# A two-layer recurrent trunk: the chunk phase's matrix products held to the program's order on TensorE

## The chip, the cores and the metric

The kernel runs on one core of a Trainium2 chip. The metric is the device time of one execution in microseconds (us), on the slowest core, which here is the only one. Five engines work beside each other: TensorE (PE, with PEld for its weight loads), VectorE (DVE), ScalarE (ACT), GpSimd (POOL) and SyncE (SP). Each executes its own list of instructions strictly in the order in which the list was built; engines wait for each other by semaphores.

## The reference, cut to what matters

Two layers over x (1024 frames of 1024 float32 values), each as x + RMSNorm(mixer(RMSNorm(x))). Layer 0 has two recurrent mixers in parallel (RG-LRU and HGRN2). Layer 1, where the change is, is RWKV-7 time mixing with 16 heads of 64:

```
r, k, v, g = projections of the mixed input        # g is the gate
decay, iclr = low-rank projections
kk = k * k_k, normalised per head;  k = k * (1 + (iclr - 1) * k_a)
for t in frames:                                   # state: 64 x 64 per head
    sa    = state @ (-kk_t)
    state = state * decay_t + sa (x) (kk*iclr)_t + v_t (x) k_t
    y_t   = state @ r_t
y = groupnorm(y) * ln_w + ln_b + bonus
out = (y * silu(g)) @ w_out                        # then RMSNorm and x +
```

## The kernel before, in words

The program runs layer 0, its output, the projections of layer 1 (r, k, v and the low-rank ones) and a preparation of the keys and queries one after the other. Then comes `chain_phase`, the last third of the time, on which the change acts. It works on 16 chunks of 64 frames and has these kinds of work, each a Python generator that issues a piece of it per step:

- **The solves** (`solve_pairs`, `invert`, lines 1294 to 1306). Each chunk needs the inverse of a triangular 64x64 matrix per head. The diagonal blocks are solved by DVE alone, by substitution: a product of a row (1294, 1303; output `PR`) and a sum (1297, 1306; output `YP`), 544 instructions in all, two pairs of chunks interleaved. They need only POOL's scaled blocks `BL`.
- **The merge** (`merge(ch)`). It joins the solved blocks: a DVE transpose (1331), 16 small PE products `pi` (1337), an ACT copy, 16 more (1346), and a DMA of the result, from which the chunk later loads its inverse `YTc` (`values(ch)`, which also loads the chunk's values into `SV`).
- **The gram products** (`gram(ch)`). Two halves, each of 8 products `pg` on PE (1415) and four masked copies on DVE, into `GM` (1420) and `RB` (1421). Then POOL scales the keys `BK` (1424), PE transposes them (`pt`, 1429) and ACT copies them out as `NK`.
- **The chain** (`chain(ch)`), the recurrence itself. Four links on PE, each of 16 products of 64x64: `pc` from `SV` and `GM` (1442), beside it `py` (1447); `pc` from the inverse and `B` (1457), after ACT has copied B; `pc` from `NK` (1464). DVE adds that to the decayed state, two instructions `SV<-pc,se` (1466), which gives the next chunk's `SV`; call that of chunk c SV(c). Then `py` from `RB` and `SV` (1469) gives the chunk's output y.
- **The gate pieces** (`pieces`, `gpiece`, `dense_n`). 32 pieces of the projection of g, of 24 products each (184 to 186, output `po`), with a sigmoid on ACT and a product on DVE (1020). They are the fill of chunks 0 to 8 and depend on nothing in the chain.
- **The output** (`project(tt)`, 1536 to 1538). 8 tiles of 128 frames, each of 2 x 24 products; they are the fill from chunk 9 on. Tile tt needs chunks 2tt and 2tt + 1, each normed (`norm`, on DVE, ACT and POOL) and turned by four PE transposes (`turn`, 1518, output `pq` or `pe`) into `yh` and `yl`.

The main loop interleaves these in the program's text: for each of a chunk's five chain steps it issues a step of the chain, 6 steps of the solves and two of merges (`background(6)`), a step of the next chunk's gram and one of the fill. From chunk 8 on the solves are all issued.

That text does not set the order on the engines. A scheduler does, when the program is built: it simulates the program, and each engine takes, among the instructions that are ready, the one with the highest priority, which is the one stated first; `high_priority(offset=100)` raises the chain and the gram from chunk 14 on, and `offset=400` the last norm and turn. An instruction that isn't ready in that simulation is overtaken by later ones that are. Where two products use the same PSUM bank in turn (`BANKS`: `pt`, `pq` and `pi` share one; `pc` has two, `py` one, `po` two, `pg` and `pe` share two), the later one waits until the earlier one has been read.

Of the kernel before, what the change touches and what calls it, by code (L numbers as in the profile page):

```python
# [16 lines left out]
P = 128  # L17
# [28 lines left out]
class Net:  # L46
# [74 lines left out]
    def weights(self, units):  # L121

        self.wp = self.ctx.enter_context(self.pool("wp", 4))
        self.order, self.queue = list(units), []

    def load_unit(self, first=False):
        nc, i = self.nc, self.order.pop(0)
# [47 lines left out]
    def dense_n(self, w, uh, ul, tt):  # L175

        nc = self.nc
        ps = self.dps()[:, 0:256]
        sl = slice(tt % 4 * P, (tt % 4 + 1) * P)
        for k in range(KT):  # L180
            a, b = uh[tt // 4][k][:, sl], ul[tt // 4][k][:, sl]
            c = slice(k % 4 * 256, (k % 4 + 1) * 256)
            h, l = w[k // 4][0][:, c], w[k // 4][1][:, c]
            nc.tensor.matmul(ps, lhsT=a, rhs=h, start=(k == 0), stop=False)  # L184
            nc.tensor.matmul(ps, lhsT=a, rhs=l, start=False, stop=False)  # L185
            nc.tensor.matmul(ps, lhsT=b, rhs=h, start=False, stop=(k == KT - 1))  # L186
        return ps

    def rstd(self, pool, ss, n, scale, eps):
# [833 lines left out]
    def chain_phase(self, cx, mp, vg, n):  # L1023


        nc, a = self.nc, self.a
        both = lambda x, y: ((x[0], y[0]), (x[1], y[1]))
        self.mp = mp
        self.psb = cx.enter_context(self.pool("psb", 1, space=PSUM))
        self.nd = 0  # L1030

        def dps():
            self.nd += 1
            return self.bank("pd" if self.nd % 2 else "pe")
# [12 lines left out]
        self.SV, self.YTc, self.G, self.Y, self.yd = {}, {}, {}, {}, [self.dram.tile([P, HALF], F32, name=f"yd{i}") for i in range(16)]  # L1047
        g0, g1 = (self.mix_parts(mp, 3, th, nc.gpsimd) for th in range(2))
        for i in range(n):
            next(vg)  # L1050
            self.background(5)
            if i >= n - 8:
                next(g0)
        self.chain_consts()
        self.values(0)
        nc.gpsimd.memset(self.SV[0][0:64, 0], 0.0)
        nc.gpsimd.memset(self.SV[0][64:128, 1], 0.0)
        for _ in self.gram(0):
            pass
        self.dps = lambda: self.bank("po")  # L1060

        def output():
            for tt in range(8):
                yield from self.project(tt)

        self.fill = self.pieces(self.gpiece, *both(g0.parts, g1.parts))
        for ch in range(16):
            gr = iter(())
            if ch == 8:
                while self.solves:  # L1070
                    self.background(8)
                ivx.close()
                self.gp = cx.enter_context(self.pool("gp", 2))
                self.output_consts()
                self.W = {}
            if ch == 9:
                self.turn(0)
                self.turn(1)
                for _ in self.fill:
                    pass  # L1080
                self.fill = output()
            if 0 < ch < 15:
                self.values(ch + 1)
                gr = self.gram(ch + 1)
            steps = self.chain(ch)
            for i in range(5):
                with self.tc.high_priority(offset=100) if ch >= 14 else ExitStack():
                    if next(steps, True) is not None:
                        break
                self.background(6)  # L1090
                if ch == 0 and i < 2:
                    for _ in range(4):
                        next(g1)
                if ch == 0 and i == 1:
# [218 lines left out]
    def merge(self, ch):  # L1313
# [20 lines left out]
        for e in range(KT):  # L1334
            for h in range(2):
                r, r2 = slice(64 * h, 64 * h + 32), slice(64 * h + 32, 64 * h + 64)
                nc.tensor.matmul(ps[r2, e, 0:32], lhsT=A12[r, e, :], rhs=X1[r, e, :], start=True, stop=True)
        for h in range(2):
            r2 = slice(64 * h + 32, 64 * h + 64)
            nc.scalar.copy(F[r2], ps[r2, :, 0:32])  # L1340
# [2 lines left out]
        for e in range(KT):  # L1343
            for h in range(2):
                r, r2 = slice(64 * h, 64 * h + 32), slice(64 * h + 32, 64 * h + 64)
                nc.tensor.matmul(ps[r, e, 0:32], lhsT=F[r2, e, :], rhs=YT[r2, e, 32:64], start=True, stop=True)
# [52 lines left out]
    def gram(self, ch):  # L1399
# [10 lines left out]
        for eg in range(2):  # L1410
            ps = [self.bank("pg").rearrange("p (q t) -> p q t", t=P) for _ in range(2)]
            for q in range(4):
                for h in range(2):
                    hs = slice(64 * h, 64 * h + 64)
                    nc.tensor.matmul(ps[h][:, q, :], lhsT=BK[hs, eg * 4 + q, :], rhs=GM[hs, h, eg * 4 + q, :],  # L1415
                                     start=True, stop=True)
            for h in range(2):
                es = slice(eg * 4, eg * 4 + 4)
# [7 lines left out]
        for eg in range(2):  # L1426
            ps = self.bank("pt").rearrange("p (q t) -> p q t", t=P)
            for q in range(4):
                nc.tensor.transpose(ps[:, q, :], BK[:, eg * 4 + q, :], self.ident)
            nc.scalar.copy(NK[:, eg * 4:eg * 4 + 4, :], ps)  # L1430
        self.G[ch] = GM, RB, NK

    def chain(self, ch):
# [5 lines left out]
        pv = lambda ps: ps.rearrange("p (e v) -> p e v", v=64)  # L1439
        ps = pv(self.bank("pc"))  # L1440
        for e, h in eh:
            nc.tensor.matmul(ps[H[h], e, :], lhsT=GM[:, h, e, 0:64], rhs=SV[:, h, e, :], start=True, stop=True)
        B = self.cc[ch % 2].tile([P, KT, 64], F32, name="B")
        nc.scalar.copy(B, ps)
        py = pv(self.bank("py"))
        for e, h in eh:
            nc.tensor.matmul(py[H[h], e, :], lhsT=GM[:, h, e, 64:128], rhs=SV[:, h, e, :], start=(e == 0), stop=False,
                             skip_group_check=True)
        if ch < 15:
            se = self.cc[ch % 2].tile([P, KT, 64], F32, name="se")  # L1450
# [3 lines left out]
        yield  # L1454
        ps = pv(self.bank("pc"))
        for e, h in eh:
            nc.tensor.matmul(ps[H[h], e, :], lhsT=YT[H[h], e, :], rhs=B[H[h], e, :], start=True, stop=True)
        for h in range(2):
            nc.scalar.copy(SV[H[h], h], ps[H[h]])
        yield  # L1460
        if ch < 15:
            ps = pv(self.bank("pc"))
            for e, h in eh:
                nc.tensor.matmul(ps[H[h], e, :], lhsT=NK[:, e, H[h]], rhs=SV[:, h, e, :], start=True, stop=True)
            for h in range(2):
                nc.vector.tensor_add(self.SV[ch + 1][H[h], h], ps[H[h]], se[H[h]])  # L1466
        yield
        for e, h in eh:
            nc.tensor.matmul(py[H[h], e, :], lhsT=RB[H[h], e, :], rhs=SV[H[h], h, e, :], start=False, stop=(e == KT - 1),
                             skip_group_check=True)  # L1470
        y = self.cc[ch % 2].tile([P, HALF], F32, name="B")
        nc.scalar.copy(y, py.rearrange("p e v -> p (e v)"))
# [37 lines left out]
    def turn(self, ch):  # L1510
# [4 lines left out]
            self.yl = self.wp.tile([P, KT, P], F32R, name="yl", tag="wl")  # L1515
        ps = self.bank("pq" if ch < 12 else "pe")
        for q in range(4):
            nc.tensor.transpose(ps[:, q * P:(q + 1) * P], y[:, q * P:(q + 1) * P], self.ident)
        T = slice(64 * p, 64 * p + 64)
        self.split(ps.rearrange("p (k t) -> p k t", t=64), self.yh[:, :, T], self.yl[:, :, T])  # L1520

    def project(self, tt):
# [8 lines left out]
        for dh in range(2):  # L1531
            ds = slice(dh * HALF, (dh + 1) * HALF)
            po = self.bank("po")
            for k in range(KT):
                h, l = self.W[k, dh]
                nc.tensor.matmul(po, lhsT=yh[:, k, :], rhs=h, start=(k == 0), stop=False)  # L1536
                nc.tensor.matmul(po, lhsT=yh[:, k, :], rhs=l, start=False, stop=False)  # L1537
                nc.tensor.matmul(po, lhsT=yl[:, k, :], rhs=h, start=False, stop=(k == KT - 1))  # L1538
# [70 lines left out]
```

## Time and profile before

| what | value |
|---|---|
| median of 3 runs | 1861.41 us (1859.28 to 1864.62) |
| the profiled execution | 1867.26 us |
| its span, first to last instruction | 1865.6 us |
| mean granted clock of TensorE | 0.948 |
| PE busy | 1714.8 us (92%) |
| DVE busy | 1326.3 us (71%) |
| ACT busy | 776.5 us (42%) |
| POOL busy | 715.7 us (38%) |

The share of an engine is its mean over the whole span; the chunk phase, from about 1330 us on, differs from the rest. A line such as "L1466" is a line of the kernel, and "SV<-pc,se" means that an instruction writes the tile SV and reads pc and se. In the rows of a timeline the first column is the start in us from the beginning of the span, the second the duration. One product of 32-bit floats is executed in several passes and can show as more than one matmul in the profile. PEclk is the clock that TensorE was granted, as a share of full speed.

### The profile page before, as it was taken

What the parts mean: (1) busy time and instruction counts of PE and PEld (TensorE: products, weight loads), DVE (VectorE), ACT (ScalarE), POOL (GpSimd) and SP (SyncE); (2) the same over time, 40 slices, a digit from 0 to 9 for tenths busy, and PEclk for the clock granted to TensorE, in tenths of its full rate; (3) what the DMA queues carried; (4) which work ended last, traced back from release to release, by engine and by line L of the source; (5) the groups of instructions that cost most, each with busy time, mean ns of one, the idle gap of its engine ahead of it and who ended that gap; (6) DMA issues with size and microseconds to landing.
All of it is one profiled execution on the core that took longest, in us unless ns stands there. A gap on an engine that the chain in (4) does not pass through costs nothing. (4 is left out here: it accounts for less than half of the span.)

```text
span 1865.6 us, 34533 instructions
## 1 busy us (share of the span) xinstructions
PE 1714.8 (92%) x13394; PEld 1436.2 (77%) x13394; DVE 1326.3 (71%) x2605; ACT 776.5 (42%) x1484; POOL 715.7 (38%) x638
## 2 busy tenths in 40 slices
PE   8989989999899999999999999979788888898988
PEld 6879879788797777777878866659787777776766
DVE  6486484685946898835445486795999999658884
ACT  5222222323136655534545565677452322342321
POOL 5533333332332122365434243466353242464440
PEclk8989999999899999999999999979889989897989
DMA  5101101111012121265242256766244544755531
GB/s 183 46 24 35 57 24 69 45 33 38 24 63 85 57 69 67 100 225 198 94 141 89 92 136 159 166 172 187 87 128 128 164 134 114 213 185 161 172 101 63
DMA packets 177492, 201.80 MB, mean 108 GB/s; under 512 B 91440, under 2 KB 122416, under 8 KB 177328
## 3 DMA queue, kind: packets, MB, share of 16 engines
q1 hardware_dynamic: 176176, 195.39, 34.1%
q0 software_dynamic: 1152, 4.19, 0.7%
q8 instruction: 106, 1.74, 0.4%
q14 instruction: 58, 0.48, 0.1%
HBM read 136.28 MB, written 63.24 MB: 107 GB/s over the span
## 5 line engine op out<-in xcount | busy, mean ns | idle before, releaser
L135 POOL TENSOR_TENSOR wl<-w,wh 128x1024 fp32r<-128x1024 f32 x110 | 275.9, 2514 | 292.4 <-ACT wh L133 277.0
L160 PE MATMUL mm<-xh,wh 128*128 128x512 f32 x768 | 305.9, 399 | 1.2 <-ACT KK L1183 1.2
L162 PE MATMUL mm<-xh,wl 128*128 128x512 f32 x768 | 304.8, 397 | 0.0
L161 PE MATMUL mm<-xl,wh 128*128 128x512 f32 x768 | 303.9, 396 | 0.0
L184 PE MATMUL mm<-wh,xh 128*128 128x256 f32 x560 | 170.5, 305 | 5.0 <-ACT xh L149 3.3
L160 PEld LDWEIGHTS mm<-xh,wh 128*128 128x128 f32 x768 | 145.4, 189 | 36.8 <-issue 3.9
L162 PEld LDWEIGHTS mm<-xh,wl 128*128 128x128 f32 x768 | 145.5, 190 | 34.9 <-issue 4.6
L161 PEld LDWEIGHTS mm<-xl,wh 128*128 128x128 f32 x768 | 145.7, 190 | 33.5 <-issue 3.6
L186 PE MATMUL mm<-wh,xl 128*128 128x256 f32 x560 | 167.0, 301 | 4.7 <-DVE xl L150 3.2
L185 PE MATMUL mm<-wl,xh 128*128 128x256 f32 x560 | 165.8, 297 | 0.0
L133 ACT CAST wh<-w 128x1024 fp32r<-128x1024 f32 x112 | 117.4, 1050 | 116.2 <-PE mm L161 55.7
L1294 DVE TENSOR_TENSOR PR<-YP,BL 128x80 f32<-128x80 f32 (+21 forms) x240 | 125.3, 544 | 14.9 <-POOL BL L1276 12.4
L184 PEld LDWEIGHTS mm<-wh,xh 128*128 128x128 f32 x560 | 114.9, 205 | 8.2 <-ACT xh L149 3.8
L186 PEld LDWEIGHTS mm<-wh,xl 128*128 128x128 f32 x560 | 114.0, 205 | 7.0 <-DVE xl L150 4.0
L185 PEld LDWEIGHTS mm<-wl,xh 128*128 128x128 f32 x560 | 115.0, 205 | 0.7
L184 PE MATMUL po<-wh,xh 128*128 128x256 f32 x256 | 80.6, 315 | 2.1 <-DVE vg L1020 2.1
L185 PE MATMUL po<-wl,xh 128*128 128x256 f32 x256 | 78.8, 308 | 0.0
L186 PE MATMUL po<-wh,xl 128*128 128x256 f32 x256 | 77.9, 304 | 0.0
L420 DVE COPY_PREDICATED ST<-m_l,sm 64x128 f32<-64x128 uint8 x224 | 72.5, 337 | 5.5
L803 DVE SCALAR_TENSOR_TENSOR mix<-ut,vec,mix 128x512 f32<-128x512 f32 x64 | 58.1, 916 | 24.2 <-ACT mix L802 23.3
L1415 PE MATMUL pg<-GM,BK 64*128 64x128 f32 x512 | 61.9, 318 | 13.9 <-DVE RB L1421 6.6
L1453 POOL TENSOR_TENSOR se<-SV,egc 64x512 f32<-64x512 f32 x30 | 33.4, 1115 | 88.6 <-DVE SV L1466 87.2
(373 smaller groups left out, 4334.0 us busy)
## 6 DMA issues: line engine op xcount, KB each, us to landing
w<-in_W SPq DMA_DIRECT2D x112, 512.0 KB, 3.6
ard<-AR SPq DMA_DIRECT2D x16, 512.0 KB, 3.7
BK<-bkd SPq DMA_DIRECT2D x16, 512.0 KB, 4.9
vd<-vg SPq DMA_DIRECT2D x32, 256.0 KB, 2.8
GM<-ard SPq DMA_DIRECT2D x32, 256.0 KB, 4.4
x<-in_x SPq DMA_DIRECT2D x8, 512.0 KB, 10.1
mgd<-sgq SPq DMA_DIRECT2D x16, 256.0 KB, 2.2
ut<-mgd SPq DMA_DIRECT2D x16, 256.0 KB, 4.0
```

Source lines behind the costliest of these rows:

```text
L133: nc.scalar.copy(hi, w)
L135: (nc.vector if first else nc.gpsimd).tensor_sub(lo, w, hi.bitcast(F32))
L160: nc.tensor.matmul(ps, lhsT=wh[:, c:c + P], rhs=a, start=(k == 0), stop=False)
L161: nc.tensor.matmul(ps, lhsT=wh[:, c:c + P], rhs=b, start=False, stop=False)
L162: nc.tensor.matmul(ps, lhsT=wl[:, c:c + P], rhs=a, start=False, stop=(k == KT - 1))
L184: nc.tensor.matmul(ps, lhsT=a, rhs=h, start=(k == 0), stop=False)
L185: nc.tensor.matmul(ps, lhsT=a, rhs=l, start=False, stop=False)
L186: nc.tensor.matmul(ps, lhsT=b, rhs=h, start=False, stop=(k == KT - 1))
L420: nc.vector.copy_predicated(d, m, x)
L803: nc.vector.scalar_tensor_tensor(out, sh, self.v(f"mu{p}", k), out, ALU.mult, ALU.add)
L1294: nc.vector.tensor_mul(pr, fv(YP, yo, kd + [[48, 8], [1, n]]), fv(BL, ao + i, k0 + [[0, 8], [32, n]]))
L1415: nc.tensor.matmul(ps[h][:, q, :], lhsT=BK[hs, eg * 4 + q, :], rhs=GM[hs, h, eg * 4 + q, :], start=True, stop=True)
```

## The change

From the end of chunk 0's gram on, every product and every transpose on TensorE goes through `self.mm` or `self.tr`, which hand the instruction to `keep_in_program_order`. That adds to it an ordering edge to the instruction that PE was given just before it: the scheduler may no longer place it ahead of that one. The edge is between instructions of one engine, so it costs no semaphore; it changes nothing but the place in the list. The other engines stay free: DVE, ACT, POOL and SP are still scheduled by priority among what is ready.

```diff
+        self.mm, self.tr = self.nc.tensor.matmul, self.nc.tensor.transpose
...
         self.dps = lambda: self.bank("po")

+        pin = self.tc.keep_in_program_order
+        self.mm, self.tr = (lambda *a, f=f, **k: pin(f(*a, **k)) for f in (nc.tensor.matmul, nc.tensor.transpose))
+
...
-            nc.tensor.matmul(ps, lhsT=a, rhs=h, start=(k == 0), stop=False)
+            self.mm(ps, lhsT=a, rhs=h, start=(k == 0), stop=False)
...
-                nc.tensor.transpose(ps[:, q, :], BK[:, eg * 4 + q, :], self.ident)
+                self.tr(ps[:, q, :], BK[:, eg * 4 + q, :], self.ident)
```

The first line stands in `weights`, the lambda in `chain_phase`, the products shown in `dense_n` and `gram`. The same replacement is made for all other products of `dense_n`, `merge`, `gram`, `chain`, `turn` and `project`. The lines of the kernel shift by one behind the first edit and by four behind the second; pinned products carry the line of the lambda, 1064.

What it moves, in the built lists (a row is an instruction or a group of like ones; a number behind a name, as in `xh_13085`, is that of a buffer).

PE, where chunk 0's chain starts, before: its products `pc` and `py` come one or a few at a time between gate pieces (`po`), a merge (`pi`) and the next gram (`pg`).

```order
L184 MATMUL po<-wh,xh_13085 128x256
L185 MATMUL po<-wl,xh_13085 128x256
L186 MATMUL po<-wh,xl_13086 128x256
L184 MATMUL po<-wh,xh_13134 128x256
L1442 MATMUL pc<-SV,GM 64x64
L1447 MATMUL py<-SV,GM 64x64
L1346 MATMUL pi<-YT_11967,A_12712 32x32 x16
L1415 MATMUL pg<-GM,BK 128x128 x4
L185 MATMUL po<-wl,xh_13134 128x256
L186 MATMUL po<-wh,xl_13135 128x256
L184 MATMUL po<-wh,xh_13183 128x256
L185 MATMUL po<-wl,xh_13183 128x256
```

The same place after: the chain's 16 products `pc` and 16 `py` stand in one piece, behind the inversion products of chunks 2 and 3 and the key transposes, and the first gate pieces of the phase come after them.

```order
L1419 MATMUL pg<-GM,BK 128x128 x4
L1341 MATMUL pi<-X_13232,A_13071 32x32 x16
L1341 MATMUL pi<-X_13234,A_13082 32x32 x16
L1350 MATMUL pi<-YT_11966,A_13071 32x32 x16
L1350 MATMUL pi<-YT_11967,A_13082 32x32 x16
L1433 MATMUL pt<-ident,BK 128x128 x8
L1064 MATMUL pc<-SV,GM 64x64 x16
L1064 MATMUL py<-SV,GM 64x64 x16
L1064 MATMUL po<-wh,xh_12925 128x256
L1064 MATMUL po<-wl,xh_12925 128x256
L1064 MATMUL po<-wh,xl_12926 128x256
```

DVE around SV(4), before: the solves' rows 1294 and 1297 stand on both sides of it (410 of the 544 ahead of it), between gate products and gram masks.

```order
L1294 TENSOR_TENSOR PR<-YP,BL 128x208
L1294 TENSOR_TENSOR PR<-YP,BL 128x40
L1020 TENSOR_TENSOR vg<-po,vg 128x256
L1297 TENSOR_REDUCE YP<-PR 128x2x8
L1297 TENSOR_REDUCE YP<-PR 128x8
L1466 TENSOR_TENSOR SV<-pc,se 64x512 x2
L1294 TENSOR_TENSOR PR<-YP,BL 128x224
L1294 TENSOR_TENSOR PR<-YP,BL 128x48
L1420 TENSOR_TENSOR GM<-pg,gm 64x512
L1421 TENSOR_TENSOR RB<-pg,gm 64x256
L1297 TENSOR_REDUCE YP<-PR 128x2x8
```

After: 543 of the 544 solve rows (1298, 1301 and their fellows) stand ahead of SV(4), and the masks follow behind the last.

```order
L1301 TENSOR_REDUCE YP<-PR 128x2x8
L1298 TENSOR_TENSOR PR<-YP,BL 128x240
L1301 TENSOR_REDUCE YP<-PR 128x2x8
L1021 TENSOR_TENSOR vg<-po,vg 128x256
L1298 TENSOR_TENSOR PR<-YP,BL 128x256
L1470 TENSOR_TENSOR SV<-pc,se 64x512 x2
L1301 TENSOR_REDUCE YP<-PR 128x2x8
L1424 TENSOR_TENSOR GM<-pg,gm 64x512
L1425 TENSOR_TENSOR RB<-pg,gm 64x256
L1424 TENSOR_TENSOR GM<-pg,gm 64x512
L1425 TENSOR_TENSOR RB<-pg,gm 64x256
```

PE ahead of the last turn, before: the last output chain `py` (1469) is followed by 48 output products, of which the first rows are shown, and then the transposes `pe<-ident,B` of chunk 15's turn.

```order
L1518 MATMUL pe<-ident,yn 128x128 x8
L1469 MATMUL py<-SV,RB 64x64 x16
L1536 MATMUL po<-xh_16588,yh 128x512
L1537 MATMUL po<-xl_16589,yh 128x512
L1536 MATMUL po<-xh_17039,yh 128x512
L1537 MATMUL po<-xl_17040,yh 128x512
L1538 MATMUL po<-xh_16588,yl 128x512
L1536 MATMUL po<-xh_16592,yh 128x512
L1537 MATMUL po<-xl_16593,yh 128x512
L1538 MATMUL po<-xh_16592,yl 128x512
```

After, from the turn of chunk 14 (`pe<-ident,yn`) on: behind `py` stand 12 output products, of which the first rows are shown, and then the turn of chunk 15.

```order
L1064 MATMUL po<-xh_17053,yl 128x512
L1064 MATMUL pe<-ident,yn 128x128 x4
L1064 MATMUL py<-SV,RB 64x64 x16
L1064 MATMUL po<-xh_17106,yh 128x512
L1064 MATMUL po<-xl_17107,yh 128x512
L1064 MATMUL po<-xh_17106,yl 128x512
L1064 MATMUL po<-xh_17110,yh 128x512
L1064 MATMUL po<-xl_17111,yh 128x512
```

The last of the twelve, and the turn:

```order
L1064 MATMUL po<-xh_17120,yh 128x512
L1064 MATMUL po<-xl_17121,yh 128x512
L1064 MATMUL po<-xh_17120,yl 128x512
L1064 MATMUL pe<-ident,B 128x128 x4
L1064 MATMUL po<-xh_16588,yh 128x512
```

Of the 48 products that stood between this `py` and the turn, 12 stand there now; the other 36 stand ahead of `py`. Behind the turn stand 48 products in both.

More of the change, by code (lines that the diff above doesn't have):

```diff
@@ L183, in dense_n @@
             h, l = w[k // 4][0][:, c], w[k // 4][1][:, c]
-            nc.tensor.matmul(ps, lhsT=a, rhs=h, start=(k == 0), stop=False)
-            nc.tensor.matmul(ps, lhsT=a, rhs=l, start=False, stop=False)
-            nc.tensor.matmul(ps, lhsT=b, rhs=h, start=False, stop=(k == KT - 1))
+            self.mm(ps, lhsT=a, rhs=h, start=(k == 0), stop=False)
+            self.mm(ps, lhsT=a, rhs=l, start=False, stop=False)
+            self.mm(ps, lhsT=b, rhs=h, start=False, stop=(k == KT - 1))
         return ps
@@ L1336, in merge @@
                 r, r2 = slice(64 * h, 64 * h + 32), slice(64 * h + 32, 64 * h + 64)
-                nc.tensor.matmul(ps[r2, e, 0:32], lhsT=A12[r, e, :], rhs=X1[r, e, :], start=True, stop=True)
+                self.mm(ps[r2, e, 0:32], lhsT=A12[r, e, :], rhs=X1[r, e, :], start=True, stop=True)
         for h in range(2):
@@ L1345, in merge @@
                 r, r2 = slice(64 * h, 64 * h + 32), slice(64 * h + 32, 64 * h + 64)
-                nc.tensor.matmul(ps[r, e, 0:32], lhsT=F[r2, e, :], rhs=YT[r2, e, 32:64], start=True, stop=True)
+                self.mm(ps[r, e, 0:32], lhsT=F[r2, e, :], rhs=YT[r2, e, 32:64], start=True, stop=True)
         for h in range(2):
@@ L1414, in gram @@
                     hs = slice(64 * h, 64 * h + 64)
-                    nc.tensor.matmul(ps[h][:, q, :], lhsT=BK[hs, eg * 4 + q, :], rhs=GM[hs, h, eg * 4 + q, :],
+                    self.mm(ps[h][:, q, :], lhsT=BK[hs, eg * 4 + q, :], rhs=GM[hs, h, eg * 4 + q, :],
                                      start=True, stop=True)
@@ L1441, in chain @@
         for e, h in eh:
-            nc.tensor.matmul(ps[H[h], e, :], lhsT=GM[:, h, e, 0:64], rhs=SV[:, h, e, :], start=True, stop=True)
+            self.mm(ps[H[h], e, :], lhsT=GM[:, h, e, 0:64], rhs=SV[:, h, e, :], start=True, stop=True)
         B = self.cc[ch % 2].tile([P, KT, 64], F32, name="B")
@@ L1446, in chain @@
         for e, h in eh:
-            nc.tensor.matmul(py[H[h], e, :], lhsT=GM[:, h, e, 64:128], rhs=SV[:, h, e, :], start=(e == 0), stop=False,
+            self.mm(py[H[h], e, :], lhsT=GM[:, h, e, 64:128], rhs=SV[:, h, e, :], start=(e == 0), stop=False,
                              skip_group_check=True)
@@ L1456, in chain @@
         for e, h in eh:
-            nc.tensor.matmul(ps[H[h], e, :], lhsT=YT[H[h], e, :], rhs=B[H[h], e, :], start=True, stop=True)
+            self.mm(ps[H[h], e, :], lhsT=YT[H[h], e, :], rhs=B[H[h], e, :], start=True, stop=True)
         for h in range(2):
@@ L1463, in chain @@
             for e, h in eh:
-                nc.tensor.matmul(ps[H[h], e, :], lhsT=NK[:, e, H[h]], rhs=SV[:, h, e, :], start=True, stop=True)
+                self.mm(ps[H[h], e, :], lhsT=NK[:, e, H[h]], rhs=SV[:, h, e, :], start=True, stop=True)
             for h in range(2):
@@ L1468, in chain @@
         for e, h in eh:
-            nc.tensor.matmul(py[H[h], e, :], lhsT=RB[H[h], e, :], rhs=SV[H[h], h, e, :], start=False, stop=(e == KT - 1),
+            self.mm(py[H[h], e, :], lhsT=RB[H[h], e, :], rhs=SV[H[h], h, e, :], start=False, stop=(e == KT - 1),
                              skip_group_check=True)
@@ L1517, in turn @@
         for q in range(4):
-            nc.tensor.transpose(ps[:, q * P:(q + 1) * P], y[:, q * P:(q + 1) * P], self.ident)
+            self.tr(ps[:, q * P:(q + 1) * P], y[:, q * P:(q + 1) * P], self.ident)
         T = slice(64 * p, 64 * p + 64)
@@ L1535, in project @@
                 h, l = self.W[k, dh]
-                nc.tensor.matmul(po, lhsT=yh[:, k, :], rhs=h, start=(k == 0), stop=False)
-                nc.tensor.matmul(po, lhsT=yh[:, k, :], rhs=l, start=False, stop=False)
-                nc.tensor.matmul(po, lhsT=yl[:, k, :], rhs=h, start=False, stop=(k == KT - 1))
+                self.mm(po, lhsT=yh[:, k, :], rhs=h, start=(k == 0), stop=False)
+                self.mm(po, lhsT=yh[:, k, :], rhs=l, start=False, stop=False)
+                self.mm(po, lhsT=yl[:, k, :], rhs=h, start=False, stop=(k == KT - 1))
                 if k == 3:
```

## Prediction

> **What bounds the kernel now.** I read the page first, then the busy time by stretch, then VectorE's timeline and groups, then TensorE's timeline for the price of one product, and last the waits. From the page: the totals, and the slices of the two busy engines and of the clock.
>
> ```profile
> PE 1714.8 (92%) x13394; PEld 1436.2 (77%) x13394; DVE 1326.3 (71%) x2605; ACT 776.5 (42%) x1484; POOL 715.7 (38%) x638
> PE   8989989999899999999999999979788888898988
> DVE  6486484685946898835445486795999999658884
> PEclk8989999999899999999999999979889989897989
> ```
>
> From slice 29 on (about 1330 us, where the chunk phase starts) PE falls to 8 and DVE rises to 9. The busy time by stretch splits this phase:
>
> ```profile
> core 0: us, PE busy (x) PEld busy (x) DVE busy (x) ACT busy (x) POOL busy (x), PEclk, DMA share, GB/s
> 1300.00:1600.00 300.00, 252.41 (x3396) 231.79 (x3396) 285.39 (x658) 106.58 (x253) 113.23 (x84) 0.90 0.46 135
> 1600.00:1700.00 100.00, 88.78 (x1102) 75.27 (x1102) 63.67 (x121) 33.45 (x68) 52.22 (x42) 0.84 0.61 182
> 1631.00:1808.00 177.00, 157.83 (x1754) 128.12 (x1748) 142.62 (x254) 53.03 (x116) 92.82 (x70) 0.90 0.51 159
> ```
>
> Until 1600 DVE is busy 285.4 of 300 us: it sets the pace. After that no engine is full: DVE has 64%, and PE's 89% hides a granted clock of 0.84. To place the chunks I use the state addition that closes chunk c, SV(c), DVE line 1466, two instructions. In order of time: SV(4), SV(6), the last solve, SV(8), SV(14).
>
> ```profile
> 1521.32 1.40 DVE L1466 TENSOR_TENSOR SV<-pc,se 64x512 f32<-64x512 f32 x2
> 1576.96 1.40 DVE L1466 TENSOR_TENSOR SV<-pc,se 64x512 f32<-64x512 f32 x2
> 1593.71 0.43 DVE L1297 TENSOR_REDUCE YP<-PR 128x16 f32<-128x256 f32 x1
> 1631.87 1.41 DVE L1466 TENSOR_TENSOR SV<-pc,se 64x512 f32<-64x512 f32 x2 [0.25 <-PE pc L1464]
> 1806.82 1.41 DVE L1466 TENSOR_TENSOR SV<-pc,se 64x512 f32<-64x512 f32 x2
> ```
>
> So the solves end between chunks 6 and 8; chunks 9 to 14 take 174.9 us (29 each), and 57.4 us follow SV(14).
>
> **The change part by part.** No instruction is added or removed on any engine (DMA issues included), and the first 7033 PE rows are the same. Everything is waiting: PE may no longer fill a wait with a later product. Two things follow, read from the order of the built programs.
>
> First, DVE's order. The solves need no product, so the scheduler moves them ahead into the time in which chunk products now stand behind each other. Of the 544 solve instructions, 410 stood ahead of SV(4) and 521 ahead of SV(6); now 543 stand ahead of SV(4). When DVE finishes the solves the recurrence is at chunk 4, not past chunk 6. DVE executes its order in full, so the time of SV(4) follows from what stands ahead of it, against what stood ahead of SV(6): 11 L1294 and 11 L1297 more; 8 L1420, 8 L1421, 7 L1020, 4 L1466 and 2 L1331 fewer. Prices, from the groups of DVE in the solving stretch:
>
> ```profile
> L1294 DVE TENSOR_TENSOR PR<-YP,BL 128x128 f32<-128x128 f32 (+20 forms) x229 | 120.9, 550 | 2.7 <-POOL BL L1276 0.4
> L1297 DVE TENSOR_REDUCE YP<-PR 128x8 f32<-128x72 f32 (+26 forms) x229 | 55.7, 264 | 2.1
> L1420 DVE TENSOR_TENSOR GM<-pg,gm 64x512 f32<-64x512 f32 x34 | 23.3, 684 | 2.1 <-PE pg L1415 1.6
> L1421 DVE TENSOR_TENSOR RB<-pg,gm 64x256 f32<-64x256 f32 x34 | 14.4, 422 | 0.8
> L1020 DVE TENSOR_TENSOR vg<-po,vg 128x256 f32<-128x256 f32 x26 | 11.0, 422 | 1.7 <-ACT vg L1019 1.3
> L1466 DVE TENSOR_TENSOR SV<-pc,se 64x512 f32<-64x512 f32 x14 | 9.6, 686 | 0.3
> L1331 DVE STREAM_TRANSPOSE X<-YT 128x256 f32<-128x256 f32 x14 | 6.1, 437 | 0.7 <-DMA YT<-xb 0.6
> ```
>
> That is +9.0 us and -15.4 us: SV(4) ends at 1578.4 - 6.4 = **1572.0**. PE's waits up to there (the first chunk's products now stand behind the inversion products of chunks 2 and 3, and behind them ACT's copy of B and SV(0)) I cost at nothing: 21 more solve instructions stand ahead of SV(0), so DVE works meanwhile. If that cover fails DVE itself idles. In the solving stretch it waited 1.6 us for gram products (GM row above); the bounds are 0 and, if that wait came at each of nine gram halves, 15 us. I take 0, since the order was made around these waits.
>
> Second, PE's order from SV(4) on. What stands behind the last product of SV(4) is, in both kernels, the same list. Unit prices at full clock are these rows: a gate piece (8 of line 186 with their 16 fellows; 96 in 34.5 us, so 2.88 us a piece), 48 output products (11.2), 16 chain products (1.1 to the next row, printed as 32 passes), 8 gram products (1.1, 16 passes), 4 transposes (0.66; a turn's the same), 16 inversion products (0.69).
>
> ```profile
> 1300.60:1335.10 34.50, 27.13 (x96) 18.37 (x96) 1.00 0.32 107
> 1834.40:1845.60 11.20, 11.16 (x48) 8.92 (x48) 0.69 (x1) 0.69 (x2) 1.00 0.27 94
> 1796.28 1.15 PE L1447 MATMUL py<-SV,GM 128*64 128x64 f32 x32
> 1797.37 1.16 PE L1415 MATMUL pg<-GM,BK 64*128 64x128 f32 x16
> 1798.46 0.66 PE L1429 MATMUL pt<-ident,BK 128*128 128x128 f32 x4
> 1640.93 0.69 PE L1337 MATMUL pi<-X,A 32*32 32x32 f32 x32
> ```
>
> SV(4) to SV(8), four chunks with hardly any DVE load: 14 gate pieces 40.3, 20 chain groups 22.0, 8 gram groups 8.8, 8 transposes in fours 5.3, 10 inversion groups 6.9: 83.3 us of PE. The chain's own links are covered: behind each stand 12 or 24 products. Not covered are the second gram half, which waits for DVE's masks of the first, and sometimes the key transposes, which wait for POOL. By these rows of the waits of PE (us in total, times, longest) that is 0.94 twice a chunk and about 0.6:
>
> ```profile
> PE pg L1415 <- DVE RB L1421: 6.6, 7, 2.3
> PE pt L1429 <- POOL BK L1424: 4.7, 2, 2.7
> PE po L1538 <- DVE yl L150: 4.4, 3, 1.5
> ```
>
> 2.5 us a chunk, 10 us: **93 us** (bounds 83 and, at the share of 22% that the last stage loses now, 107; the waits of PE are nearest). SV(8) at 1665, 32 us later than now.
>
> SV(8) to SV(14): PE needs 5.5 output tiles 61.6, 30 chain groups 33, 12 gram groups 13.2, 24 transposes in fours 15.8, 2 gate pieces 5.8, 4 inversion groups 2.8: 132.2 us, 22.0 a chunk. DVE has 257 instructions there; at 142.62/254 = 0.561 us (third stretch above) 144.3 us. It also waits for ACT within each row norm, by these rows 0.73 us at 12 squares and 0.25 us at 18 square roots, 13 us:
>
> ```profile
> DVE va L1503 <- ACT sq L1501: 5.1, 7, 0.8
> DVE rr L203 <- ACT rr L202: 1.5, 6, 0.3
> ```
>
> DVE ends last: **158 us** (bounds 144, all of it covered, and 175, as now). This stage gains 17 us: chain, gram and norm now come at an even distance, where before PE ran chunks 9 and 10 ahead and then did output products for long. SV(14) at 1823.
>
> SV(14) to the end: 120 output products 28.0, 5 chain groups 5.5, gram 1.1, 24 transposes 4.0: 38.6 us. Line 1447's chain of chunk 15 is no longer pulled ahead, so only 12 output products (2.8 us) cover norm(15), where 48 do now. Norm(15) runs from the first row below to the end of the second, 7.8 us with 2.8 us of other work in it; with the copies around it PE waits about 5 us for the last turn. Two waits for yl (row above) add 3 us, and behind PE stand 7.5 us to the end of the span, as now.
>
> ```profile
> 1835.42 0.69 DVE L1498 TENSOR_REDUCE m<-B 128x8 f32<-128x512 f32 x1
> 1842.54 0.68 DVE L1507 TENSOR_TENSOR B<-B,V 128x512 f32<-128x512 f32 x1
> 1858.09 0.60 ACT L1545 ACTIVATE o<-po 128x512 f32<-128x512 f32 x1 [4.30 <-PE po L1538]
> ```
>
> **54 us** (57.4 now; bounds 47 without waits, 60).
>
> Sum: 1572 + 93 + 158 + 54 = 1877 us of span against 1865.6: **+12 us**. The profiled execution took 1867.3 us, 5.9 over the median of the runs, so 1879 on its own scale and **1873 us** on that of the median, 0.6% slower.
>
> **The rivals.** *The clock falls in the new waits.* PE's price doubles at half clock. In the trace a half-clock stretch began behind two waits of 2.06 and 1.35 us (the first two rows; the third is the stretch):
>
> ```profile
> 1719.24 0.46 PE L1415 MATMUL pg<-GM,BK 64*128 64x128 f32 x2 [2.06 <-issue]
> 1721.05 0.80 PE L1538 MATMUL po<-xh,yl 128*128 128x512 f32 x1 [1.35 <-DVE yl L150]
> 1720.40:1727.20 6.80, 6.15 (x15) 4.86 (x16) 5.99 (x9) 0.63 (x1) 2.41 (x2) 0.50 0.37 125
> ```
>
> 15 products in 6.15 us are 0.41 us each against 0.23, so such a stretch loses 2.9 us. One in each of ten chunks adds 29 us: 1902 us on the median's scale. For it: the waits that I forecast have this size. Against it: the even order leaves no long hole before the last turn. The Trainium skill's page "TensorE: Matmul & The Clock Gate" (Part 1, the table of the two states) says that the clock halves after at least one idle window of about 3.4 us. By that rule waits of 1 to 2 us would cost only themselves and this rival would be worth nothing but a stretch at the last turn; the row above disagrees in so far as the two waits were each shorter.
>
> *The stated order flows (faster).* The mechanism is in chunks 9 to 14: if DVE fills ACT's answers with the other row norm, as its new order interleaves two, the stage takes 144; with 84 and 52 for the stages around it the sum is 1852, so 1848 us. It decides once the waits behind SV(4) come to 18 us less than I count. For it: the same list of products took 343 us behind SV(4) before, and its bare price is 255. Against it: two whole chunks must be won back after the solves.
>
> *The two cancel.* Behind at 1572 by two chunks, won back by the even order to within 5 us: it takes about 150 us for chunks 9 to 14 and one wait fewer elsewhere: 1862 us. That the change does nothing is excluded, since the order differs.
>
> **How the numbers follow.** A difference under 0.3% (5.6 us) can't be told from none. Forecast, 1867 to 1892: 0.50. Clock, 1892 to 1925: 0.17. Cancel, 1856 to 1867: 0.18. Flow, 1835 to 1856: 0.15. So faster 0.15, same 0.18, slower 0.67. The range, with about 0.1 left on each side, is 1852 to 1905; the forecast's own is 1867 to 1892.
>
> **What would show it.** DVE at 94% or more until the last solve; SV(4) near 1572 with it; PE's busy time before SV(4) lower by some 40 us (two chunks of products); SV(8) near 1665, SV(14) near 1823; a wait of some 5 us before the last turn. Wrong if DVE idles within the solves (then worse), if chunks 9 to 14 take under 24 us each (then faster), or if the clock in them falls under 0.9.

## The result, and the profile after

The changed kernel is slower: 1924.74 us median (1921.76 to 1926.33) against 1863.01 us for the kernel before on the same chip, a ratio of 1.032 (95% interval 1.029 to 1.036). The forecast was 1873 us, in a range of 1852 to 1905: the direction was right, the size a fifth of what came.

The page of the changed kernel, the same lines as before:

```profile
span 1924.1 us, 34500 instructions
PE 1693.2 (88%) x13394; PEld 1427.3 (74%) x13394; DVE 1298.2 (67%) x2605; ACT 779.6 (41%) x1484; POOL 714.9 (37%) x638
PE   8989999899999999999999999797577685868887
DVE  6484582767847889464463867949999954347764
PEclk9999999999999999999999999899688887989998
```

The span grew by 58.5 us, but PE's 13394 matmul records took 21.6 us less in total (1693.2 against 1714.8). So PE stands idle 80 us more: 230.9 us instead of 150.8 (span less busy). Its row falls to 5, 7 and 6 in slices where it had 7 to 8. The same by stretch, each kernel cut at 1325 us, at the ends of its own SV(0), SV(4), SV(8) and SV(14), and at PE's last product; first before, then after:

```profile
1325.00:1421.40 96.40, 77.49 (x846) 71.46 (x844) 92.91 (x196) 41.21 (x96) 41.83 (x29) 0.84 0.40 118
1421.40:1522.70 101.30, 81.42 (x1283) 72.53 (x1283) 95.84 (x226) 27.82 (x56) 37.85 (x29) 0.91 0.47 130
1522.70:1633.30 110.60, 95.56 (x1451) 87.05 (x1450) 90.32 (x214) 34.48 (x72) 41.50 (x36) 0.89 0.59 171
1633.30:1808.20 174.90, 155.53 (x1707) 126.00 (x1705) 141.01 (x251) 52.87 (x115) 90.70 (x68) 0.90 0.50 158
1808.20:1858.10 49.90, 48.95 (x284) 35.85 (x284) 25.61 (x60) 11.26 (x29) 3.82 (x3) 0.97 0.20 67
```

```profile
1325.00:1419.10 94.10, 54.93 (x685) 50.97 (x683) 90.70 (x199) 39.53 (x91) 43.38 (x30) 0.71 0.40 114
1419.10:1561.20 142.10, 104.46 (x1536) 96.25 (x1536) 137.56 (x350) 32.39 (x67) 40.64 (x32) 0.83 0.38 108
1561.20:1681.50 120.30, 88.47 (x1340) 81.84 (x1341) 42.35 (x84) 32.85 (x66) 43.95 (x38) 0.84 0.51 149
1681.50:1865.90 184.40, 148.09 (x1699) 121.84 (x1697) 126.22 (x259) 53.95 (x118) 80.74 (x61) 0.91 0.46 149
1865.90:1916.60 50.70, 40.21 (x292) 31.75 (x292) 20.25 (x50) 10.94 (x25) 5.62 (x4) 0.83 0.16 55
```

In each row the first number is the length, the second PE's busy time; their difference is PE's idle time. It was 18.9, 19.9, 15.0, 19.4 and 1.0 us before and is 39.2, 37.6, 31.8, 36.3 and 10.5 now: every stage lost 9.5 to 20 us. To SV(4), behind which the same products are left in both kernels, the lag is 38.5 us (1561.2 against 1522.7); chunks 5 to 8 add 9.7, chunks 9 to 14 add 9.5, the rest 0.8.

What PE waits for, from the same 1325 us on; first before, then after, the largest rows and those to compare (us in total, times, longest):

```profile
PE pi L1337 <- DVE X L1331: 12.6, 3, 8.6
PE pc L1442 <- DVE GM L1420: 11.5, 6, 4.2
PE pg L1415 <- DVE RB L1421: 6.6, 7, 2.3
PE pt L1429 <- POOL BK L1424: 4.7, 2, 2.7
PE pt L1429 <- ACT NK L1430: 2.3, 2, 1.5
```

```profile
PE pg L1064 <- DVE RB L1425: 32.4, 13, 10.7
PE pt L1064 <- POOL BK L1428: 28.6, 10, 5.6
PE pi L1064 <- ACT A L1344: 18.3, 6, 12.2
PE pi L1341 <- DVE X L1335: 14.9, 2, 9.4
PE pi L1064 <- ACT YT L1353: 11.7, 6, 7.4
PE pt L1064 <- ACT NK L1434: 10.1, 15, 0.7
```

The two largest waits of before did not grow: that for X came from 12.6 to 14.9 us (products of line 1341, stated ahead of the pin), and that of the chain for GM fell to 0.9 us. What grew are the waits of the other small products: gram for RB from 6.6 to 32.4 us, key transposes for BK from 4.7 to 28.6, and those of the merges for ACT. Behind most of them stand gate or output products that need nothing late.

One such wait followed to its end, chunk 5. On DVE the first instruction of norm(0) had moved ahead of SV(5); DVE stood 9.06 us for its rows, which come by DMA, and SV(5), whose product had ended at 1583.5, stands behind it. ACT's square for the same norm stands ahead of the copy that an inversion product on PE needs. The copy also stands behind the square of the second norm, which waits for DVE, and behind the load of ACT's table for a root (1.28 us); so the wait for data is the first part of PE's 12.16 us and not all of them. DVE, then ACT, then PE:

```profile
1590.64 0.69 DVE L1502 TENSOR_REDUCE m<-yn 128x8 f32<-128x512 f32 x1 [9.06 <-DMA yn<-yd]
1592.29 1.40 DVE L1470 TENSOR_TENSOR SV<-pc,se 64x512 f32<-64x512 f32 x2
```

```profile
1592.41 0.63 ACT L1505 ACTIVATE sq<-yn 128x512 f32<-128x512 f32 x1 [9.55 <-DVE yn L1503]
1598.10 0.63 ACT L1505 ACTIVATE sq<-yn 128x512 f32<-128x512 f32 x1 [4.79 <-issue]
1598.74 1.28 ACT L203 ACT_TABLE_LOAD   x1
1600.75 0.74 ACT L1344 COPY A<-pi 32x256 f32<-32x256 f32 x2
```

```profile
1582.37 1.15 PE L1064 MATMUL pc<-SV,NK 128*64 128x64 f32 x32
1601.54 1.07 PE L1064 MATMUL pi<-X,A 32*32 32x32 f32 x32 [12.16 <-ACT A L1344]
```

And the wait that returns in each of chunks 10 to 14 (1.49 to 4.84 us), here chunk 13: POOL scales the keys only after two decays that wait for SV and after an addition of a norm (`V`), and PE waits 3.55 us, with 12 output products behind the transposes in its list. In chunk 11, where the scaling stands ahead of that addition, PE waits 1.49 us.

```profile
1809.72 2.15 POOL L1457 TENSOR_TENSOR se<-SV,egc 64x512 f32<-64x512 f32 x2 [0.23 <-DVE SV L1470]
1811.95 1.27 POOL L1498 TENSOR_TENSOR V<-V,ln 128x512 f32<-128x512 f32 x1
1813.17 1.90 POOL L1428 TENSOR_TENSOR BK<-BK,egc 128x1024 f32<-128x1024 f32 x1
```

```profile
1815.13 0.66 PE L1064 MATMUL pt<-ident,BK 128*128 128x128 f32 x4 [3.55 <-POOL BK L1428]
```

### The profile page after: what moved, and what is told of

Read it like the earlier page. It is cut to its first block, busy times and chain, and to the rows that moved or that the text cites. A ratio compares the mean times of both kernels' runs of the same rounds, so it can differ in the third digit from the quotient of the medians.

```text
span 1924.1 us, 34500 instructions
## 1 busy us (share of the span) xinstructions
PE 1693.2 (88%) x13394; PEld 1427.3 (74%) x13394; DVE 1298.2 (67%) x2605; ACT 779.6 (41%) x1484; POOL 714.9 (37%) x638
## 5 line engine op out<-in xcount | busy, mean ns | idle before, releaser
L1298 DVE TENSOR_TENSOR PR<-YP,BL 128x80 f32<-128x80 f32 (+21 forms) x240 | 116.9, 509 | 14.3 <-POOL BL L1280 12.0
L1064 PE MATMUL po<-wh,xh 128*128 128x256 f32 x256 | 84.8, 331 | 4.4 <-DVE vg L1021 4.4
L1064 PE MATMUL pg<-GM,BK 64*128 64x128 f32 x480 | 45.4, 317 | 33.8 <-DVE RB L1425 32.4
L1020 ACT ACTIVATE vg<-po 128x256 f32<-128x256 f32 x32 | 12.3, 383 | 135.1 <-PE po L1064 125.5
```

The source lines that it names most:

```text
L1064: self.mm, self.tr = (lambda *a, f=f, **k: pin(f(*a, **k)) for f in (nc.tensor.matmul, nc.tensor.transpose))
L1298: nc.vector.tensor_mul(pr, fv(YP, yo, kd + [[48, 8], [1, n]]), fv(BL, ao + i, k0 + [[0, 8], [32, n]]))
```

## The experiments

Theory 1: the lag comes from VectorE's order. The solves moved ahead of the chain's additions, and the chain is two chunks late when they end. Theory 2: it comes from TensorE's waits. Held in order, it stands at a product whose operand is late, with other work ready behind it. All ratios are against the kernel before on the same chip, with 95% intervals; idle is the span of the profiled execution less PE's busy time (150.8 us before, 230.9 after).

| experiment | ratio | interval | idle, us |
|---|---|---|---|
| the change | 1.032 | 1.029 to 1.036 | 230.9 |
| 1 held from chunk 9 | 1.005 | 1.003 to 1.007 | 167.7 |
| 2 held to chunk 8 | 1.030 | 1.026 to 1.033 | 198.4 |
| 3 fill free | 1.008 | 1.005 to 1.011 | 184.2 |
| 4 solves behind the chain | 1.027 | 1.024 to 1.030 | 214.8 |
| 5 norms late | 1.025 | 1.021 to 1.029 | 222.0 |
| 6 keys first | 1.030 | 1.027 to 1.032 | 224.8 |
| 7 merges free | 1.018 | 1.015 to 1.020 | 198.4 |
| 8 products in the wait | 1.033 | 1.031 to 1.036 | 219.1 |
| 9 chain products added to the last tile | 1.037 | 1.035 to 1.040 | 230.2 |
| 10 held from 9, fill ahead of the keys | 1.003 | 1.002 to 1.005 | 168.6 |
| 11 four waits taken out together | 1.020 | 1.018 to 1.022 | 208.7 |
| 12 fill free, norms late, solves behind | 1.015 | 1.014 to 1.017 | 200.4 |
| 13 fill alone held | 1.004 | 1.002 to 1.006 | 155.4 |
| 14 held from chunk 1 | 1.031 | 1.029 to 1.033 | 224.0 |
| 15 before, chunk 15 in groups | 0.999 | 0.998 to 1.001 | 153.0 |
| 16 fill and merges free | 1.005 | 1.003 to 1.007 | 180.7 |

### Where: 1 and 2

Experiment 1 moves the two lines of the pin from the end of chunk 0's gram into `if ch == 9:`; experiment 2 leaves them and ends the pin there:

```diff
             if ch == 9:
+                self.mm, self.tr = nc.tensor.matmul, nc.tensor.transpose
                 self.turn(0)
```

> The products are held to the stated order only from chunk 9 on; chunks 0 to 8 are as before. The changed kernel was 48 us behind at SV(8) and lost another 10 us by the end. If the loss belongs to the solving stage (theory 1: VectorE's order, which puts the solves ahead of the chain), this kernel has SV(8) at 1633 us as before and ends within 6 us of before, 1857 to 1869 us. If each wait at a held product costs its own length (theory 2), chunks 9 to 14 cost the 184 us of the changed kernel against 175 before: 1869 to 1876 us. If the stated output stage were the main loss, over 1890 us.

> The products are held up to the end of chunk 8 and free from chunk 9 on. SV(8) should be at 1681 us as in the changed kernel. Theory 1 and theory 2 both expect the free output stage to take the 175 us and 57 us of before, no more: 1908 to 1918 us. If a free TensorE could win back the lag with output products, under 1895 us.

Measured: 1.005 and 1.030. Chunks 0 to 8 carry nearly all of it. The 1872 us of experiment 1 lie in the range of theory 2; the 1920 us of experiment 2 lie a little above what both expected. Experiment 1 had SV(8) at 1630 us, like before; chunks 9 to 14 took 182.3 us against 174.9, and the end came 3 us late in the profiled execution. In experiment 2 the free output stage took 175.9 us, so free output products don't win the lag back.

### Which relation: 3, 7, 13, 16

A selective pin: a product whose output is in `free` takes no edge, the others get theirs to the last held one.

```diff
-        pin = self.tc.keep_in_program_order
+        def pin(ins):
+            if last[0] is not None:
+                self.tc.add_manual_dep(ins.ins, last[0], <NoSync>)
+            last[0] = ins.ins.name
+            return ins
...
+        free = ("po",)        # 3; ("pi",) in 7; all but "po" in 13; ("po", "pi") in 16
```

> The gate products and the output products are free again; the chain, gram, merge, transposes keep the stated order among themselves. Theory 2 (TensorE stands at a late operand with other work ready behind): fill enters the waits, TensorE's idle time falls from 155 us after 1325 us to under 100, and the time to 1860 to 1885 us. Theory 1: VectorE's order still has 513 of the 544 solve instructions ahead of SV(4), the chain is as late as in the changed kernel, 1905 to 1925 us.

> The changed kernel with the inversion products pi free, all others held among themselves. They waited some 50 us in the changed kernel (for ACT's A and YT and VectorE's X). Theory 2: 1890 to 1905 us. If only the fill matters, since a free pi lets no fill pass, 1915 to 1925 us.

> Only the gate and output products are held, among themselves; chain, gram, merge and transposes are free. VectorE's order is that of before up to the solves. If the loss comes from fill that may not pass a waiting small product (theory 2), holding fill alone costs nothing: 0.997 to 1.004 of before, 1860 to 1872 us. If holding as such costs (the scheduler's freedom in fill matters), over 1.01.

> Gate products, output products and inversion products free; gram, chain, key transposes and turns held among themselves. Freeing fill alone gave 1.008 of before, freeing the merges alone 1.018. Theory 2 (what may pass a wait decides): 1.000 to 1.006. If the waits left are those of gram and transposes among themselves: 1.006 to 1.012.

Measured: 1.008, 1.018, 1.004 and 1.005. The four times are those of theory 2. Freeing the gate and output products (3) takes away three quarters of the loss, while VectorE's order still has 513 of the 544 solve instructions ahead of SV(4) (410 before). With the merges free too (16) it is 0.5% at 462 instructions; the intervals of 3 and 16 overlap, so that the merges add to it is not shown. PE's idle time in experiment 3 fell by 47 us only; from 1325 us on it stayed above the 100 us that were expected. Holding fill among itself costs 0.4%, the upper end of what was expected. So the loss is in the relation between the two kinds, since either kind held among itself costs under 1%. The pin forbids both directions, and no run takes one away alone. That it is fill that may not pass a waiting small product, and not a small product that may not pass fill, is argued from PE's 80 us of new idle time: behind fill PE would be busy. In experiment 3 the chain is as late as in the changed kernel, SV(4) at 1562.9 us, but PE did 192 us of work since 1325 instead of 159:

```profile
1325.00:1562.90 237.90, 192.34 (x2501) 178.46 (x2501) 230.94 (x531) 79.65 (x176) 98.72 (x74) 0.86 0.45 129
```

A late chain as such was not what cost; the products that PE had not done meanwhile were.

### VectorE's order: 4

```diff
-                nc.vector.tensor_mul(pr, fv(YP, yo, ...), fv(BL, ...))
+                behind(nc.vector.tensor_mul(pr, fv(YP, yo, ...), fv(BL, ...)))    # and the other solve instructions
...
+        def behind(ins):       # a NoSync edge to the latest SV addition stated ahead
+            if getattr(self, "lastsv", None):
+                self.tc.add_manual_dep(ins.ins, self.lastsv, <NoSync>)
```

> The changed kernel, with each solve instruction held behind the latest SV addition stated ahead of it: 456 of 544 solve instructions stand ahead of SV(4) and 504 ahead of SV(5), against 543 and 544. Theory 1: the chain is one and a half chunks further when the solves end, SV(6) at 1580 to 1600 us instead of 1630, and the time 1880 to 1900 us. Theory 2: TensorE's own waits set the pace of the chain, VectorE idles instead, SV(6) at 1620 or later, 1910 to 1930 us.

Measured: 1.027, SV(4) at 1541.6 us, 20 earlier, but SV(6) at 1609.0 and SV(8) at 1671.7, 10 earlier than in the changed kernel. Theory 1 explains some 10 us of the 60; its expectation of 1880 to 1900 us failed. The time, 1915 us, is that of theory 2, but its SV(6) at 1620 us or later did not come either.

### Single waits: 5, 6, 10, and together: 11, 12

```diff
-        nc.vector.tensor_reduce(m, g3(y), AX.X, ALU.add)
+        (self.tc.keep_in_program_order if ch < 2 else lambda i: i)(nc.vector.tensor_reduce(m, g3(y), AX.X, ALU.add))
```

```diff
-                nc.gpsimd.tensor_mul(se[H[h]], SV[H[h], h], eg)
+                ins = nc.gpsimd.tensor_mul(se[H[h]], SV[H[h], h], eg)
+                self.tc.add_manual_dep(ins.ins, self.bki[ch], <NoSync>)      # bki[ch]: the scaling of BK
```

```diff
+                if i == 3 and ch > 8:                   # 10: ahead of the key transposes
+                    next(self.fill, None)
                 with self.tc.high_priority(offset=100) if ch >= 14 else ExitStack():
                     next(gr, None)
```

> The changed kernel, with the first VectorE instruction of norm(0) and norm(1) held behind everything stated before it, so that both stand behind SV(7) and no longer ahead of SV(5) and SV(6). In the changed kernel VectorE waited 9.06 us for the first of them (its rows come by DMA), SV(5) came 9 us after its product, and an inversion product on TensorE waited 12.16 us. Theory 2 (each such wait of TensorE costs its length): SV(5) at about 1585 us, SV(8) at 1668 to 1674, the time 1910 to 1917 us. Rival (the next late operand takes the wait's place): 1920 to 1928 us.

> The changed kernel, with POOL's scaling of the keys BK ordered ahead of the decay of the state (se) of the same chunk. The key transposes waited 28.6 us in all for BK, 3.55 us a chunk in chunks 10 to 14, because BK stood behind two se of 1.04 us that wait for SV. Theory 2: this wait falls under 10 us, a chunk from 27.2 to 24 or 25 us, the time 1900 to 1908 us. Rival (another engine sets the length of a chunk, the wait moves to it): 1918 to 1926 us.

> The products held from chunk 9 on, as in the first experiment (1.0046 of before), and in these chunks the 12 output products that stood behind the key transposes now stand ahead of them. Theory 2: they cover 3 of the 3.55 us that the transposes wait for BK, 2.5 to 3 us a chunk in six chunks: 15 to 18 us less, 1848 to 1856 us, faster than before. Rival (the wait moves to the gram products or the turn behind it): 1862 to 1872 us.

> The changed kernel with four causes of waits taken out together: pi free, norm(0) and norm(1) late, the solves behind the chain, and the fill ahead of the key transposes. Alone the first three gave 27, 13 and 9 us. If the waits add up (theory 2), 1860 to 1880 us; if each hides another, 1885 to 1905 us.

> Gate and output products free, the others held (1.008 of before), with norm(0) and norm(1) late and the solves behind the chain. If the waits of chunks 4 to 8 that are left (32 us idle) are those of the norms and of the solves: 1860 to 1870 us, equal to before. If they are another's: 1875 to 1885 us.

Experiment 5 did what it should: SV(5) at 1585.0 us, the stretch to SV(8) 114.7 us instead of 120.3, ratio 1.025. Of the 8.7 us that SV(5) came earlier, 3.6 were left at SV(8) (1677.9 us, where 1668 to 1674 were expected), so part of the wait moved instead of going. In experiment 6 BK stood ahead of `se`, but behind an addition of a norm's `V` on POOL: the wait for BK fell from 28.6 to 16.4 us only, and the ratio to 1.030, inside the interval of the change. That is the rival's time. In experiment 10 the transposes had their cover, and the wait came back under another name (the total, then DVE's read of the bank and the transposes in one chunk):

```profile
PE pt L1080 <- DVE rv L202: 23.9, 5, 5.7
1738.90 0.68 DVE L151 TENSOR_TENSOR yl<-pq,yh 128x512 fp32r<-128x512 f32 x1
1739.73 1.09 PE L1080 MATMUL pt<-ident,BK 128*128 128x128 f32 x4 [5.70 <-DVE rv L202]
```

They share a PSUM bank with the turn (`pq`). The fill brings the next turn with it, which now stood directly ahead of them, and DVE reads that bank behind the small steps of a norm. The ratio, 1.003, does not differ from experiment 1's; the forecast of a gain was wrong. Experiment 11 took out four causes and came to 1.020, no better than the merges alone in experiment 7 (1.018); 12 was slower than 3 (1.015 against 1.008) and above both of its expectations; why stays open. The single gains don't add. So theory 2 holds in that the waits which fill may not enter make the loss (3, 13, 16); it fails in that each wait taken out would give its length back (6, 10, 11).

### The start: 14

The two lines of the pin stand at the head of `ch == 1`.

> The products are held from chunk 1 on instead of from the end of chunk 0's gram. In the changed kernel TensorE idled 38.8 us between 1325 us and SV(0), 18.9 before, since the merges of chunks 0 to 3 stood there without a gate piece behind them that might pass. Theory 2: these 20 us come back and stay, 1900 to 1908 us (1.018 to 1.023 of before). If they are lost again later, because VectorE's order keeps 513 solve instructions ahead of SV(4): 1915 to 1925 us.

Measured: 1.031. PE did 66.9 us of work between 1325 us and SV(0) instead of 54.9, but SV(4) came at 1560.9 and SV(8) at 1682.8, as in the changed kernel. What was won at the start was lost again by SV(4), so here too a shorter wait did not stay won.

### The clock: 8

```diff
+            for _ in range(16 if ch > 9 and eg == 0 else 0):
+                self.mm(ps[:, 0, :], lhsT=self.ident, rhs=self.ident, start=True, stop=True)
             for q in range(4):
                 self.tr(ps[:, q, :], BK[:, eg * 4 + q, :], self.ident)
```

> The changed kernel with 16 more products of the identity ahead of the first key transpose of chunks 10 to 15, into the bank that the transposes then overwrite; they need nothing that is late and fill some 2.3 us of the wait of 3.55 us for BK. If the wait costs more than its length because the clock falls behind it (the transposes behind it took 1.12 us instead of 0.66, the next 12 output products 4.17 instead of 2.8): 9 us less, 1912 to 1918 us. If it costs its length only: 1922 to 1928 us. If the products delay the chain: more.

The stretch with the 12 output products behind the transposes of chunk 13, in the changed kernel and then with the wait filled:

```profile
1817.10:1821.30 4.20, 4.20 (x16) 3.37 (x15) 1.37 (x3) 1.11 (x2) 0.88 (x1) 0.68 0.35 129
```

```profile
1822.80:1825.80 3.00, 3.00 (x16) 2.42 (x15) 1.38 (x2) 0.59 (x1) 0.00 (x0) 1.00 0.74 247
```

Filled, the clock stays at 1.00 and the products take 3.0 instead of 4.2 us. The time did not fall (1.033): the sixteen products took 3.84 us, longer than the wait, and the transposes started 4.4 us behind the last chain product instead of 3.55. So the clock adds some 1.2 us behind this wait, and this experiment can't say what it adds to the whole.

### Products of two kinds in turn: 9 and 15

Experiment 9 adds 48 chain products to the last output tile; nothing reads their result.

```diff
+            if tt == 7 and dh == 0:
+                for _ in range(24):
+                    one()             # self.mm(small[...], lhsT=GM[...], rhs=SV[...])
             for k in range(KT):
...
+                    if tt == 7 and dh == 1:
+                        one()         # behind each output product
```

> The changed kernel with 48 more products in its last output tile, whose result nobody reads: 24 chain products (py from SV and GM) in one piece ahead of the first 24 output products, and 24 more one by one behind each of the second 24. In the kernel before, a chain product and an output product in turn took 0.69 us a pair (chunk 15), while 0.07 and 0.23 us are the prices in one piece. If the change of the kind of product costs time, the piece takes 1.6 + 5.6 us and the mixed half 16 us or more at full clock; if not, both halves take the same, 7.2 us.

```profile
1904.10:1906.50 2.40, 2.40 (x50) 2.33 (x49) 0.69 (x1) 0.59 (x1) 0.00 (x0) 0.61 0.03 7
1906.50:1912.30 5.80, 5.80 (x27) 4.58 (x25) 0.00 (x0) 0.04 (x1) 0.00 (x0) 1.00 0.00 0
1912.38:1928.50 16.12, 16.12 (x72) 8.86 (x71) 0.69 (x1) 0.71 (x3) 0.00 (x0) 1.00 0.00 0
```

In one piece 24 chain and 24 output products took 2.4 us (at a clock of 0.61) and 5.8; in turn, at full clock, 16.1: 0.67 us a pair where 0.30 is the price apart. This can explain why PE's busy time fell in the changed kernel. From 1325 us on the kernel before changes some 200 times between a gate or output product and another kind, the changed one some 120 times; at 0.18 us a change, half of what a pair costs more, that would be 14 of the 21.6 us, an estimate. Between products of any two kinds, told apart by their output, the traces have some 430 changes before and 230 after; what a change between two small kinds costs was not measured.

Experiment 15 tries to have that without the waits, on the kernel before:

```diff
+            if ch == 15:
+                pin = self.tc.keep_in_program_order
+                self.mm, self.tr = (lambda *a, f=f, **k: pin(f(*a, **k)) for f in (nc.tensor.matmul, nc.tensor.transpose))
...
-                if i < 3 or ch % 2 == 0 or ch > 8:
+                if (i < 3 or ch % 2 == 0 or ch > 8) and (ch, i) != (15, 2):
...
             self.norm(15)
-            self.turn(15)
+        next(self.fill, None)
+        with self.tc.high_priority(offset=400):
+            self.turn(15)
```

> The kernel before, with the products held in chunk 15 alone and 12 output products moved behind its last chain link, so that 24 cover the last norm. In the kernel before the chain of chunk 15 alternates one by one with output products (0.69 us a pair against 0.30 apart): SV(14) to the end of TensorE took 49.9 us, of which 10 are these changes. Held in groups they should be saved, but the last turn waits some 3 us: 44 to 47 us, 0.997 to 0.999 of before. If the mixing hides waits that then appear: 1.000 to 1.002.

```profile
1804.70:1854.90 50.20, 44.48 (x288) 35.03 (x288) 25.79 (x60) 12.49 (x30) 4.15 (x3) 0.90 0.19 66
```

```profile
PE pe L1073 <- DVE rv L202: 2.3, 1, 2.3
```

Measured: 0.999 (0.998 to 1.001), no difference. The expected 44 to 47 us did not come. PE's work from SV(14) to its end fell from 48.95 to 44.5 us, but 5.7 us of waits came in its place, the largest wholly in this stretch that of the last turn, 2.3 us: 50.2 us against 49.9. The granted clock was also lower there, 0.90 against 0.97, behind a wait of 5.56 us of the key transposes that ended in its first microsecond. So the slow mixed products seem to have filled waits. None of the versions beats the kernel before.

## Why the prediction was wrong

- **The solves.** Right in kind. DVE was busy 90.7 of 94.1 and 137.6 of 142.1 us until SV(4), the last solve ended with it, and PE's busy time from 1325 to 1561.2 us was 159.4 us, against this row of the kernel before, 34 less (some 40 forecast):

```profile
1325.00:1561.20 236.20, 193.74 (x2673) 175.97 (x2672) 226.09 (x526) 78.52 (x173) 91.88 (x67) 0.88 0.45 129
```

  SV(4) came at 1561.2, not 1572.0. From 1325 us on DVE was busy 228.3 us up to there, against 242.9 up to SV(6) in the kernel before: 14.6 us less where the sum had 6.4, and it idled 2.6 us less. Experiment 3 shows that the lag of the chain at this point, on which the forecast was built, was not by itself the loss.
- **SV(4) to SV(8), 93 us: the term that failed first.** It took 120.3. PE's work was 88.5 us (83.3 forecast); its waits were 31.8 us where 10 were counted. The 10 came from the waits of the trace before (0.94 us twice a chunk, 0.6 for keys). Those rows show what was left after the scheduler had put other products into each wait; they are no price for a PE that may not do that. The largest waits of this stretch now:

```profile
PE pi L1064 <- ACT A L1344: 13.6, 2, 12.2
PE pt L1064 <- POOL BK L1428: 7.5, 2, 5.6
PE pg L1064 <- DVE RB L1425: 6.9, 2, 3.8
```

  The gram halves and key transposes, the two kinds that were counted, waited 14.4 us for RB and BK. The inversion products, which the list of what is "not covered" left out and the sum put at nothing, waited 13.6 us for A. "Hardly any DVE load" was right (42.4 us busy), and still DVE made others wait, since it stood for data itself. The chain's own links were covered, as forecast: no wait of a `pc` product stands among the rows of this stretch.
- **SV(8) to SV(14), 158 us: "DVE ends last".** It took 184.4, 26 more. DVE was busy 126.2 us for 259 instructions, 0.49 us each and not 0.56, and idle 58. So DVE did not end last: PE's list has 148.1 us of work (132.2 priced at full clock, granted 0.91) and 36.3 us of waits, which the sum left out since it took DVE to hide them. The even distance between chunks did come, but only from SV(10) on (26.9 to 28.1 us a chunk; 26.3 forecast); the two chunks before that took 40.8 and 34.0.
- **SV(14) to the end, 54 us.** 58.2 (57.4 before). The wait for the last turn was 6.1 us, 5 forecast; that it was followed by half clock was not in the sum.
- **The sum.** -10.8, +27.3, +26.4 and +4.2 make the 47.1 us between 1877 and 1924.1.
- **The rivals.** "The clock falls in the new waits" had 1902 us and came in part: the clock does fall, from 0.948 to 0.930 on average. In the rows by stretch, PE's busy time times the share of the clock that was not granted is some 47 us before and 68 after, an estimate. So the clock cost PE some 20 us more at most, where PE's idle time grew by 80; it adds to the loss and is not the main cause. "The stated order flows" and "the two cancel" did not come: no chunk was won back.

The bound of 107 us for SV(4) to SV(8) and of 175 for the stage after were also short: both were drawn from what the kernel before lost with its freedom.

## What to carry to other kernels

Take the freedom to reorder from an engine, and the waits that other work had filled stand open; the wait rows of the free schedule show only what could not be filled, so price the new order from when each operand is ready on the other engines. Their in-order lists count too: an instruction that waits for a DMA ahead of one that the chain needs passes its wait on. Expect no sum of single repairs: where a product waits for several things, the next one takes over, and a free order for the independent fill was worth more here (1.008) than four repairs together (1.020).

## What the runs showed of the hardware

- Two kinds of products in turn on TensorE (128x64 chain products of two records and 128x512 output products) took 0.67 us a pair at full clock, against 0.30 in pieces of one kind.
- The clock fell behind short waits too. In the changed kernel's chunk 1, waits of 0.84, 2.00 and 0.55 us within 5 us ended a stretch at full clock (first row) and were followed by one at 0.57:

```profile
1446.30:1450.60 4.30, 1.46 (x68) 1.24 (x65) 4.26 (x11) 1.45 (x4) 0.00 (x0) 1.00 0.01 4
1450.60:1458.60 8.00, 7.45 (x42) 6.90 (x42) 7.86 (x32) 0.00 (x0) 1.37 (x2) 0.57 0.15 50
```

  By the Trainium skill's page "TensorE: Matmul & The Clock Gate" (Part 1, the table of the two states) the clock halves after at least one idle window of about 3.4 us. The wait of 3.55 us ahead of the key transposes fits it; these three, each shorter, do not, unless short stretches of work between them don't count.
